# First two experts as 96 float32 slots, one gather per 128 slots, slot counts by rank and 8 KB weight runs in a mixture-of-experts layer

## The chip, the core and the metric

The kernel runs on one core of one Trainium2 chip. The core has five engines that work side by side: TensorE (PE, with its weight loads PEld), VectorE (DVE), ScalarE (ACT), GpSimd (POOL) and SyncE (SP), and 16 DMA engines that move data between the chip's memory and the on-chip buffers. SP issues the plain transfers here, POOL the indirect ones. The metric is the device time of one execution in microseconds (us); lower is better. Each time given is a median of several executions.

## What is computed

One layer on 512 tokens of width D = 1024 in float32: a convolution and a gated linear attention with a layer norm, then a mixture of 16 experts in 4 groups, then a second layer norm. Each token takes the best group, and in it the two best experts, with weights from two softmaxes; an expert is a gated network of hidden width 512.

```python
D_MODEL = 1024; SEQ = 512; N_GROUPS = 4; EXPERTS_PER_GROUP = 4
TOP_K_IN_GROUP = 2; D_EXPERT = 512
def modulate(x, shift, scale):
    return x * (1.0 + scale) + shift
def post_norm_residual(x, y, gate, g, b):
    return layer_norm(DEEPNORM_ALPHA * x + gate * y, g, b)
# of a layer: x = post_norm_residual(x, <mixer>, ...), then
# h = modulate(x, shift2, scale2);  y = sum over a token's two experts e of
#     weight_e * ((silu(h @ w1[e]) * (h @ w3[e])) @ w2[e])
# x = post_norm_residual(x, y, gate2, ln2_g, ln2_b)
```

With the inputs of the reference the 16 experts receive 73, 3, 53, 71, 100, 186, 70, 94, 134, 56, 61, 109, 5, 5, 3 and 1 of the 1024 token places. Experts 0 and 1 are always done first; the other fourteen, sorted by their counts (rank 0 is the fullest), have 186, 134, 109, 100, 94, 71, 70, 61, 56, 53, 5, 5, 3 and 1.

## The kernel before, in words

The first half of the kernel (convolution, attention, first norm, up to about 318 us) is the same in both kernels apart from small loads. The part in question has three stages.

**Routing** (lines 1040 to 1180). DVE works out each token's group, experts and weights; a short product counts the tokens of each expert and gives every token its place in its expert's list (`pos`, `posr`). A *job* is one expert with a fixed number of *slots* (`CAPS`, by rank). For a block of slots `one_hot` builds on DVE a 0/1 matrix of tokens by slots, `slots` multiplies it on PE with a small table `aux` (tile `psl`), which gives each slot its token's row number and weight, and `gather` lets POOL fetch the tokens' rows from memory (`tokd` into `gx`). The first job is another case: `pick` brings its rows to their slots with 64 float32 products on PE with a float32 one-hot (`ohf`), without a gather. Meanwhile the weights of the first two experts come in, and `split` (line 377) cuts them into a high half (`whi`, a cast on ACT, L389) and a low half (`wlo`, a subtraction on DVE or POOL, L391).

**Jobs**, in the order F0, F1 (experts 0 and 1, 128 slots each) and then ranks 12, 0, 11, 6, 10, 1, 3, 8, 4, 2, 5, 9, 7, 13 (`ORDER`). An expert's weights are six pieces of 1 MB (two halves each of w1, w3 and w2), in a ring of twelve buffers. `ev = nc.sync.value_load(...)` reads which expert has the rank, then SP issues six loads; a load waits until the job that used its buffer is through. A job of 128 or more slots is a `BigJob`: rows are transposed on PE, scaled and shifted on DVE and ACT, split into halves (`Xh`, `Xl`), and each product is done as three (high by high, low by high, high by low) with 256 columns in w1 and w3 and 512 in w2. A job of 64 or 32 slots is a `SmallJob` of R = 2 or 4: the columns are spread over R groups of output partitions, in plain float32, without a split. Each block's output is added to its tokens' rows in memory by one indirect transfer on POOL (`scatter`, L1182, `ob` into `yd`); rows of `x1` were put in `yd` before. The loop does `hidden` of a job, the one-hots of a later one, `load` (transposes) of the next, `prep_next` (slots and gather) of the job three on, and then `outputs` (w2 and scatter).

Slots in use beyond a job's count are handled by a loop at the end (`nfb` blocks); with the counts above it has none to do, by either kernel's table.

**Tail**: `finish` reads `yd` back (`yf`), does the second norm, and stores. A scheduler orders the instructions of each engine by dependences and priorities, so the order on an engine is not quite that of the code.

## Time and profile before

| | us |
|---|---|
| Time before, median of 3 runs (702.49 to 704.54) | 704.35 |
| The profiled execution, time | 701.98 |
| The profiled execution, span of the trace | 700.2 |
| from the first product of an expert to the last (343.4 to 670.1) | 326.7 |
| from there to the end | 30.1 |

Times on the trace count from the start of the span; the profiled execution's own time is 1.8 us over its span, and the median of the runs is 2.4 us over that. In the page's first line, a share is the busy time of an engine in the span; the line of DMA gives tenths of the 16 engines' time in 40 slices of 17.5 us each. PEclk is the clock that TensorE was granted, as a share of the full one.

### The profile page before, as it was taken

To read this page: it belongs to the slowest core of one execution; us is meant where nothing else is said; L and a number is where in the kernel's file an instruction comes from. 1 tells how busy PE (TensorE), PEld (TensorE's weight loads), DVE (VectorE), ACT (ScalarE), POOL (GpSimd) and SP (SyncE) were. 2 spreads that over 40 slices of the span, in tenths; PEclk is the share of its full clock that TensorE was granted. 3 is DMA by queue.
4 is the path that set the end of the run, shared out by engine and by line. 5 is a ranking of instruction groups with operands and counts; after the bars stand their busy time and mean duration, and the time that the engine had idled before them with its cause. 6 is when DMAs were issued, how large, how long until landed. Compare 5 with 4: busy or idle time off the path is not lost.

```text
span 700.2 us, 11612 instructions
## 1 busy us (share of the span) xinstructions
PE 645.3 (92%) x4378; PEld 505.8 (72%) x4378; DVE 474.9 (68%) x1036; ACT 318.5 (45%) x505; POOL 135.2 (19%) x106
## 2 busy tenths in 40 slices
PE   5899999989999999996798899998999999999973
PEld 4565689777887787784698598594988588996431
DVE  8545741785965877649899875586669887594245
ACT  3338721458432234325276553454557375471100
POOL 2410000000000100025417312032123221122112
PEclk9999999999999999997799999999999999999998
DMA  8997965372112189626469899899999999979943
GB/s 310 370 338 248 313 197 176 121 230 73 59 62 64 57 294 373 204 91 219 165 204 355 314 338 369 263 369 353 359 367 319 324 369 345 348 216 349 318 142 116
DMA packets 114125, 176.79 MB, mean 252 GB/s; under 512 B 3905, under 2 KB 82129, under 8 KB 114066
## 3 DMA queue, kind: packets, MB, share of 16 engines
q1 hardware_dynamic: 107570, 157.31, 65.4%
q0 software_dynamic: 5136, 15.50, 8.9%
q10 hardware_dynamic: 1360, 3.21, 1.2%
q8 instruction: 36, 0.59, 0.3%
q14 instruction: 23, 0.19, 0.1%
HBM read 160.92 MB, written 15.07 MB: 251 GB/s over the span
## 4 chain that ended last, share of the span: by engine, by line
PE 68%; DVE 17%; ACT 6%; DMA 4%; issue 3%; POOL 1%; DVEq 0%; ACTq 0%
PE pb L144 32%; PE mm L144 21%; PE gl L144 3%; PE pt L154 3%; DVE wlo L391 3%; DMA raw<-in_expert_w_dram 3%; ACT whi L389 2%; PE po L144 2%; PE bg L146 2%; PE tp L154 1%; DVE gg L621 1%; PE pt L144 1%; PE py L144 1%; PE pu L144 1%; DVE gg L620 1%
## 5 line engine op out<-in xcount | busy, mean ns | idle before, releaser
L391 DVE TENSOR_TENSOR wlo<-raw,whi 128x1024 fp32r<-128x1024 f32 x65 | 80.3, 1245 | 50.9 <-ACT whi L389 50.4
L144 PE MATMUL pb<-whi,Xh 128*128 128x256 f32 x384 | 110.6, 289 | 3.7 <-ACT Xh L1205 3.7
L144 PE MATMUL pb<-whi,Xl 128*128 128x256 f32 x384 | 110.2, 288 | 1.6 <-DVE Xl L1206 1.6
L144 PE MATMUL pb<-wlo,Xh 128*128 128x256 f32 x384 | 108.9, 285 | 0.0
L389 ACT CAST whi<-raw 128x1024 fp32r<-128x1024 f32 x68 | 70.9, 1049 | 57.6 <-PE mm L144 26.2
L389 ACT CAST whi<-ew 128x1024 fp32r<-128x1024 f32 x68 | 71.3, 1051 | 29.4 <-PE pb L144 28.2
L144 PEld LDWEIGHTS pb<-whi,Xh 128*128 128x128 f32 x384 | 73.3, 191 | 8.0 <-ACT Xh L1205 7.1
L391 DVE TENSOR_TENSOR wlo<-ew,whi 128x1024 fp32r<-128x1024 f32 x56 | 68.8, 1237 | 12.9 <-ACT whi L389 10.9
L144 PEld LDWEIGHTS pb<-whi,Xl 128*128 128x128 f32 x384 | 73.1, 191 | 2.0 <-DVE Xl L1206 2.0
L144 PEld LDWEIGHTS pb<-wlo,Xh 128*128 128x128 f32 x384 | 73.3, 191 | 0.1
L1182 POOL DMA_INDIRECT yd<-ob,idx x18 | 30.6, 1699 | 103.3 <-DVE ob L1340 31.5
L391 POOL TENSOR_TENSOR wlo<-ew,whi 128x1024 fp32r<-128x1024 f32 x12 | 29.9, 2501 | 86.9 <-issue 70.2
L144 PE MATMUL mm<-hhi,whi 128*128 128x512 f32 x112 | 44.3, 403 | 1.6 <-ACT hhi L368 1.6
L144 PE MATMUL mm<-hhi,wlo 128*128 128x512 f32 x112 | 42.8, 392 | 0.0
L144 PE MATMUL mm<-hlo,whi 128*128 128x512 f32 x112 | 42.5, 390 | 0.0
L294 POOL TENSOR_TENSOR ss<-ss,nhalf 128x4 f32<-128x4 f32 x4 | 5.4, 1357 | 188.8 <-DVE ss L293 188.8
L144 PE MATMUL pb<-wlo,Ah 128*128 128x512 f32 x96 | 38.6, 403 | 0.2 <-DVE wlo L391 0.2
L144 PE MATMUL pb<-whi,Ah 128*128 128x512 f32 x96 | 38.8, 404 | 0.0
L144 PE MATMUL pb<-whi,Al 128*128 128x512 f32 x96 | 38.1, 402 | 0.3 <-DVE Al L1206 0.3
L144 PE MATMUL mm<-wlo,hhi 128*128 128x256 f32 x128 | 36.9, 288 | 0.0
L144 PE MATMUL mm<-whi,hhi 128*128 128x256 f32 x128 | 36.7, 287 | 0.0
L144 PE MATMUL mm<-whi,hlo 128*128 128x256 f32 x128 | 36.6, 286 | 0.0
(418 smaller groups left out, 1445.8 us busy)
## 6 DMA issues: line engine op xcount, KB each, us to landing
ew<-in_expert_w_dram SPq DMA_DIRECT2D x64, 1024.0 KB
raw<-in_expert_w_dram SPq DMA_DIRECT2D x32, 1024.0 KB
raw<-in_w_ada_dram SPq DMA_DIRECT2D x22, 1024.0 KB
raw<-in_w_in_dram SPq DMA_DIRECT2D x10, 1024.0 KB
raw<-in_w_out_dram SPq DMA_DIRECT2D x4, 1024.0 KB
xz<-in_x_dram SPq DMA_DIRECT2D x4, 512.0 KB
ada<-in_w_ada_dram SPq DMA_DIRECT2D x2, 1024.0 KB
x<-in_x_dram SPq DMA_DIRECT2D x4, 512.0 KB
```

The source lines that it names most:

```text
L144: return PE.matmul(o, lhsT, rhs, **kw)
L146: return PE.matmul(o, lhsT, rhs, **kw)
L154: PE.transpose(pool_tile[:, j * P:(j + 1) * P], s, ident)
L294: pows.append(G.tensor_tensor(dst, dst, nhalf[:, :dst.shape[1]], op=OP.pow))
L389: S.copy(hi, r[:, k0:k0 + step, :])
L391: lows.append(lo_eng[k0 // step].tensor_tensor(lo, r[:, k0:k0 + step, :], hi.bitcast(FT), op=OP.subtract))
L620: V.tensor_tensor_scan(g[0:DK, :], mask[0:DK, :n], m[0:DK, :], 0.0, op0=OP.mult, op1=OP.add)
L621: V.tensor_tensor_scan(g[DK:P, ::-1], mask[DK:P, :n], m[DK:P, ::-1], 0.0, op0=OP.mult, op1=OP.add)
L1182: G.indirect_dma_start(out=yd.rearrange("t (r w) -> (t r) w", r=R), out_offset=bass.IndirectOffsetOnAxis(ap=idx[:, :1], axis=0), in_=o, in ...
```

## The change

The change touches the expert part in these ways.

- The first two experts have 96 slots, done as a 64-slot part (R = 2) and a 32-slot part (R = 4) in plain float32; `FirstJob`, `pick` and their splits are gone, and so is POOL's share of the low halves (`POOL_LO`).
- The slot counts by rank go from 256, 256, 256, 128 (four times), 64 (five times), 32, 31 to 256, 192, 128 (three times), 96 (twice), 64 (three times), 32 (three times), 31. In blocks: 12 of 128 slots, 5 of 64 and 2 of 32 become 6 of 128, 8 of 64 and 8 of 32. Jobs whose weights are split go from nine to five.
- Rows come by one gather of whole 4 KB token rows for up to 128 slots, into one of three fixed buffers (`gxs`). After the first two, empty slots hold a row number beyond the table and are skipped. A `SmallBlock` gets the row numbers and weights of its R parts by a small product (`tables`, tile `ptb`).
- A piece of weights is cut so that each partition reads one run of 8 KB; before, a run was 1 KB in w1 and w3 and 4 KB in w2. The contraction index that a partition holds changes with it; transposes take every fourth column (`every`) and the modulation uses a permuted table (`abx`). Products with w1 and w3 are 512 columns wide.
- Jobs run in the order F0, F1, 12, 0, 11, 1, 9, 2, 8, 3, 7, 4, 5, 6, 10, 13. `hidden` is cut into steps; the loop does `load` of the next job ahead of the last step, then `gate` (the activation), `slots` and gather of the job two on, the first step of the next job, and then `outputs` of this one. The rows of the second norm are read at the end into the ring.

```diff
 NS = 2
-CAPS = [256] * 3 + [128] * 4 + [64] * 5 + [32, 31] + [0] * 2
-ORDER = [12, 0, 11, 6, 10, 1, 3, 8, 4, 2, 5, 9, 7, 13]
+FIRST = 96
+CAPS = [256, 192] + [128] * 3 + [96] * 2 + [64] * 3 + [32] * 3 + [31] + [0] * 2
+ORDER = [12, 0, 11, 1, 9, 2, 8, 3, 7, 4, 5, 6, 10, 13]
...
     def piece_src(nm, ev, h):
         src = a[nm][0, ev:ev + 1] if isinstance(ev, int) else a[nm][0, bass.ds(ev, 1)]
-        src = src[:, h * 256:(h + 1) * 256, :] if nm == "expert_w2" else src[:, :, h * 256:(h + 1) * 256]
-        return src.rearrange("o (k p) n -> p (o k) n", p=P)
-
-    RING = ["h8"] * 4 + ["mw"] * 2 + ["raw"] * 4 + ["h8"] * 4 + ["ew"] * 2 + ["mw"] * 2 + ["raw"] * 4
+        n = src.shape[1] // 2
+        src = src[:, h * n:(h + 1) * n, :]
+        return src.rearrange("o (p k) n -> p (o k) n", p=P)
+
+    RING = ["h8"] * 4 + ["mw"] * 2 + ["raw"] * 4 + ["ew"] * 2
...
-        shape = [P, 2, 1024] if nm == "expert_w2" else [P, 8, 256]
-        r = raw8(shape) if tag == "raw" else (e8 if tag == "ew" else h8 if tag == "h8" else m8)(shape, FT, "ew")
+        r = ring_tile([P, 2, 1024] if nm == "expert_w2" else [P, 4, 512])
...
-    V.memset(e0c[:, 0:NS], float(P))
+    V.memset(e0c[:, 0:NS], float(FIRST))
...
-    def gather(idx, R):
-        g = mo.tile([P, D // R], FT, name="gx", tag="gx", bufs=3)
-        ins = G.indirect_dma_start(out=g, out_offset=None, in_=tokd.rearrange("t (r w) -> (t r) w", r=R),
-                             in_offset=bass.IndirectOffsetOnAxis(ap=idx[:, :1], axis=0))
-        return g, ins
...
+    class Group:
...
+            self.n = sum(P // R for R, _ in blocks)
+            self.blocks = [(Block if R == 1 else SmallBlock)(self, R, o) for R, o in blocks]
...
+            pa = pt_("psl")
+            for i in range(NT):
+                mm(pa[:n, :NA], self.oh[:, i, :n], self.auxj(i), start=i == 0, stop=i == NT - 1)
...
+            self.g = gxs[ngx[0] % len(gxs)][:n]
+            ngx[0] += 1
+            kw = dict(bounds_check=T - 1, oob_is_err=False) if ngx[0] > NS else {}
+            self.last = G.indirect_dma_start(out=self.g, out_offset=None, in_=tokd,
+                                             in_offset=bass.IndirectOffsetOnAxis(ap=idx[:, :1], axis=0), **kw)
...
+                for c in range(4):
+                    PE.transpose(pt[:, c * n:(c + 1) * n], every(gh, 4, c), ident[:n, :n])
...
+                    A, B = (abx[:, q, ks, 0:1].to_broadcast([P, 4, n]) for q in range(2))
+                    x = self.xt[:, ks, :n]
+                    V.tensor_tensor(x, v, A, op=OP.mult)
+                    V.tensor_tensor(x, x, B, op=OP.add)
...
+            xh, xl = self.group.X
+            for k in range(4):
+                kc = 4 * c + k
+                mm3(self.H[wi], xh[:, kc, :], xl[:, kc, :], his[k], los[k], kc == 0, kc == KC - 1)
...
+            for k in range(4):
+                for q in range(R):
+                    wi, part_ = divmod(q, gw)
+                    mm(self.ph[q * n:(q + 1) * n, :w], self.group.xt[:, 4 * c + k, self.o:self.o + n],
+                       wts[2 * c + wi][:, k, part_ * w:(part_ + 1) * w],
+                       start=c == 0 and k == 0, stop=c == 1 and k == 3)
...
+    def parts_of(cap):
+        groups, off = [], 0
+        while off < cap:
+            R = next(R for R in (1, 2, 4) if P // R <= cap - off or R == 4)
+            if off % P == 0:
+                groups.append([])
+            groups[-1].append((R, off % P))
+            off += P // R
+        return groups
...
+            for c in range(2):
+                for wi in range(2):
+                    if self.big:
+                        W = split(wts[2 * c + wi], 512)
+                        for b in self.big:
+                            b.products(c, wi, *W)
+                        yield
+                if self.small:
+                    for b in self.small:
+                        b.products(c, wts)
...
-    def pick(hf):
-        pt, grp = pt_(), Bank()
-        for k in range(4):
-            for i in range(NT):
-                ks = slice((4 * hf + k) * P, (4 * hf + k + 1) * P)
-                grp.mm(pt[:, k * P:(k + 1) * P], x1[i][:, ks], ohf[:, i, :])
-        x0b.append(pt)
...
+    for j in seq[:NS]:
+        ohs[j] = hots(j)
+        warm(WARM2, pt_)
+        prep(j)
+    jobs[seq[0]].load()
+    with tc.issue_after(jobs[seq[NS - 1]].last.ins):
+        for g, n in zip(gxs, [FIRST] * NS + [0]):
...
+    for i in range(NT - 2, NT):
+        with tc.issue_after(jobs[seq[NS - 1]].last.ins):
+            G.tensor_tensor(x1[i], x1[i], l1g, op=OP.mult)
+        nc.sync.dma_start(yd[i * P:(i + 1) * P, :], x1[i])
+    load_first(6 * NS)
...
+    run = {seq[0]: jobs[seq[0]].hidden(wts[seq[0]])}
+    next(run[seq[0]])
     for n_, j in enumerate(seq):
...
-        jobs[j].hidden(wts[j])
+
+        rest = range(jobs[j].steps - 1)
+        for q in rest:
+            if q == rest[-1] and jn is not None:
+                jobs[jn].load()
+            next(run[j])
...
-        if n_ + 1 < len(seq):
-            jobs[seq[n_ + 1]].load()
-        prep_next(n_ + 3)
+        jobs[j].gate()
+        if n_ >= NS:
+            jobs[j].tables()
+        if n_ + 3 < len(seq) and n_ + 3 >= NS + 2:
+            ohs[seq[n_ + 3]] = hots(seq[n_ + 3])
+        if n_ + 2 < len(seq) and n_ + 2 > NS:
+            prep(seq[n_ + 2])
...
+        if jn is not None:
+            run[jn] = jobs[jn].hidden(wts[jn])
+            next(run[jn])
...
+        if jn is not None:
             jobs[j].outputs(wts[j])
```

(`.n` is the number of slots of a group; `xt` are the modulated rows, transposed; `gxs` are the three buffers of rows. `ptb` stands in `SmallBlock.table`, which copies the result to a weight and a row number.)

On POOL, at the end of routing (L391 before is the low half of a first expert's weights; L1177 and, after, L1227 are gathers; L1182 and L1187 are scatters), before:

```order
L391 TENSOR_TENSOR wlo<-ew,whi 128x1024 x4
L1177 DMA gx<-tokd,idx 128x1024
L1392 MEMSET mark 128x1
L1454 TENSOR_TENSOR x_2369<-x_2369,l1g 128x1024 x2
L1177 DMA gx<-tokd,idx 128x256
```

and after:

```order
L1227 DMA gx_3110<-tokd,idx 96x1024
L1227 DMA gx_3111<-tokd,idx 96x1024
L1476 MEMSET gx_3110 32x1024
L1476 MEMSET gx_3111 32x1024
L1476 MEMSET gx_3112 128x1024
L1483 COPY rep_3201<-ident 64x128 x2
L1483 COPY rep_3204<-ident 32x128 x4
L1488 MEMSET mark 128x1
L1496 TENSOR_TENSOR x_2394<-x_2394,l1g 128x1024 x2
L1227 DMA gx_3112<-tokd,idx 32x1024
```

The four subtractions are gone from the routing, two gathers stand in their place, and buffers are cleared behind them.

On the same queue, where the first two jobs put their outputs out, before:

```order
L1177 DMA gx_3257<-tokd_2403,idx_3253 128x256
L391 TENSOR_TENSOR wlo_3567<-raw_2911,whi_3566 128x1024
L1182 DMA yd_2404<-ob_3535,idx_3168 640x1024
L391 TENSOR_TENSOR wlo_3600<-raw_2913,whi_3599 128x1024
L1177 DMA gx_3478<-tokd_2403,idx_3475 128x1024
L1177 DMA gx_3491<-tokd_2403,idx_3488 128x1024
```

and after:

```order
L1187 DMA yd_2429<-ob_3457,idx_3213 1280x512
L1187 DMA yd_2429<-ob_3477,idx_3219 2560x256
L1227 DMA gx0_3110<-tokd_2428,idx_3576 128x1024
L1227 DMA gx1_3111<-tokd_2428,idx_3590 128x1024
L1187 DMA yd_2429<-ob_3622,idx_3225 1280x512
L1187 DMA yd_2429<-ob_3642,idx_3231 2560x256
```

Each of the first two jobs now has two scatters, and the gathers of rank 0 stand behind the first pair.

On PE, where a job of 128 slots follows one of 64 (`psl` is the product that gives slots their row numbers, `pt<-ident,gx` are the transposes of gathered rows, products with `Ah` and `Al` are the outputs of the job before the two, `xt` and `at` those of the job of 64), before, about the job of rank 6:

```order
L144 MATMUL psl<-aux,oh 128x6
L144 MATMUL pb<-whi,Ah 128x512
L144 MATMUL pb<-wlo,Ah 128x512
...
L144 MATMUL pb<-raw,xt 64x256 x19
L154 MATMUL pt<-ident,hs 128x128 x2
L144 MATMUL pb<-raw,xt 64x256 x13
L144 MATMUL pb<-ew,at 64x512
L154 MATMUL pt<-ident,hs 128x128 x2
L154 MATMUL pt<-ident,gx 128x128 x4
```

and after, about the job of rank 3 (between the two parts stand the 24 output products of rank 2):

```order
L144 MATMUL psl<-aux,oh 128x6
L144 MATMUL pb<-whi,Ah 128x512
L144 MATMUL pb<-wlo,Ah 128x512
...
L144 MATMUL pb<-whi,Al 128x512
L1253 MATMUL pt<-ident,gx_3112 128x128 x8
L144 MATMUL pb<-ew,xt 64x512 x7
```

Before, the row numbers in these rows are for jobs behind rank 6, whose own rows were gathered a stage earlier; after, they are rank 3's own, and 24 products stand between them and the transposes.

## Rows read from the trace of the kernel before

**Rows 1.** The page: busy time of the engines, DMA by slice, and the DMA queues.

```profile
PE 645.3 (92%) x4378; PEld 505.8 (72%) x4378; DVE 474.9 (68%) x1036; ACT 318.5 (45%) x505; POOL 135.2 (19%) x106
...
DMA  8997965372112189626469899899999999979943
...
q1 hardware_dynamic: 107570, 157.31, 65.4%
q0 software_dynamic: 5136, 15.50, 8.9%
```

**Rows 2.** Stages: start:end us, length, busy us by engine (count), PE clock, DMA share, GB/s.

```profile
343.40:371.10 27.70, 23.05 (x159) 20.79 (x157) 25.74 (x61) 19.60 (x33) 7.89 (x4) 0.94 0.76 264
371.10:394.90 23.80, 21.18 (x142) 18.23 (x143) 23.04 (x38) 14.24 (x17) 15.70 (x7) 0.93 1.07 361
394.90:403.00 8.10, 7.23 (x108) 3.88 (x107) 6.02 (x18) 3.69 (x9) 2.60 (x2) 1.00 0.69 244
403.00:440.20 37.20, 36.98 (x269) 33.95 (x270) 24.89 (x49) 17.78 (x27) 7.73 (x5) 1.00 1.07 358
440.20:453.80 13.60, 13.57 (x93) 6.88 (x92) 5.93 (x11) 5.10 (x11) 1.57 (x1) 1.00 0.85 234
618.50:636.90 18.40, 18.40 (x135) 16.52 (x133) 15.76 (x23) 10.65 (x13) 5.71 (x4) 1.00 1.00 294
636.90:649.20 12.30, 12.27 (x90) 6.66 (x91) 2.61 (x6) 1.30 (x4) 1.70 (x2) 1.00 1.06 352
662.90:670.10 7.20, 6.02 (x99) 3.10 (x98) 1.20 (x3) 1.88 (x4) 1.55 (x1) 1.00 0.39 61
670.10:700.20 30.10, 15.69 (x32) 6.57 (x32) 17.03 (x33) 2.17 (x3) 6.01 (x7) 0.84 0.38 141
```

**Rows 3.** Timeline of DVE in the routing: start us, us, engine, line, operation, tiles.

```profile
321.21 2.06 DVE L1060 TENSOR_TENSOR e1e<-e1e,e1k 128x16 f32<-128x16 f32 x1
326.81 2.33 DVE L1127 CAST aux<-wgt 128x8 bf16<-128x8 f32 x1
329.05 2.44 DVE L1154 TENSOR_SCALAR ohf<-slot,posr 128x128 f32<-128x128 bf16 x1
```

**Rows 4.** Timeline of POOL: start us, us, engine, line, operation, tiles, [idle before, releaser].

```profile
326.64 7.07 POOL L391 TENSOR_TENSOR wlo<-ew,whi 128x1024 fp32r<-128x1024 f32 x3 [3.41 <-ACT whi L389]
...
445.69 1.57 POOL L1182 DMA_INDIRECT yd<-ob,idx  x1 [8.41 <-DMA yd<-ob,idx]
...
457.68 1.48 POOL L1177 DMA_INDIRECT gx<-tokd,idx  x1 [0.30 <-PE pb L144]
```

**Rows 5.** Timeline of PE, at the first job and at rank 1.

```profile
333.99 5.52 PE L144 MATMUL pt<-ohf,x 128*128 128x128 f32 x26 [1.65 <-DVE ohf L1154]
343.44 0.36 PE L144 MATMUL pb<-whi,Xh 128*128 128x256 f32 x1
...
488.88 0.60 PE L154 MATMUL pt<-ident,gx 128*128 128x128 f32 x4
```

**Rows 6.** The gathers (tile gx), time from issue to landing.

```profile
DMA to landing us min/median/max: 4.3/8.2/11.4
```

**Rows 7.** PE groups by form in job 12: form xcount, busy us, mean ns, idle before.

```profile
L144 PE MATMUL pb<-ew,xt 128*32 128x256 f32 x64 | 3.7, 380 | 0.0
L144 PE MATMUL pb<-ew,at 128*32 128x256 f32 x32 | 2.1, 385 | 0.1
```

**Rows 8.** The scatters (line 1182), time from issue to landing.

```profile
DMA to landing us min/median/max: 5.0/9.2/10.9
```

**Rows 9.** DMA from 511 to 520 us, with weights in 1 KB runs alone.

```profile
DMA packets 3102, 3.14 MB, mean 349 GB/s; under 512 B 48, under 2 KB 3101, under 8 KB 3101
```

**Rows 10.** DMA from 521.5 to 526.5 us, with weights in 4 KB runs.

```profile
DMA packets 565, 2.04 MB, mean 408 GB/s; under 512 B 29, under 2 KB 80, under 8 KB 565
```

**Rows 11.** The chain that ended last: start us, us, what.

```profile
664.02 4.96 DMA yd<-ob,idx
668.99 3.86 DMA yf<-yd
```

476 lines of the change are left out of this document (245 added, 231 removed).

## The prediction

> **What bounds the kernel now.** I read the page first, then the stages of the expert part, then the timelines at its start, and the chain at its end. In the page TensorE is busy for 92% of the span, and the slices of DMA are nearly all 9 in the last half [rows 1]. Two resources are thus close to full, and the table by stage says which one sets the end of each stage [rows 2]. In the second job DVE is busy for 23.04 of 23.8 us: the halves of the weights are the limit there. In rank 0 (256 slots, 403.0 to 440.2) PE is busy for 36.98 of 37.2 us, in rank 5 (618.5 to 636.9) for 18.40 of 18.40, in rank 9 (636.9 to 649.2) for 12.27 of 12.3. From rank 0 on PE is the bound, and DMA runs close beside it (share 1.07 in the first of these). So what takes work from PE is worth its full time, as long as DMA doesn't become the limit: the ring is twelve pieces deep, and a job's own weights were loaded two jobs ahead.
>
> Ahead of the jobs, DVE works through the routing. Three of its instructions there take 2.06, 2.33 and 2.44 us [rows 3], where others of the same lines take 0.17 to 0.3; each lies beside POOL's subtractions, of which three take 7.07 us together [rows 4]. The first job's rows then come to their slots by float32 products on PE, the last 26 of them 5.52 us long, and the first product of an expert starts at 343.44 [rows 5].
>
> **Start of the jobs.** POOL's subtractions leave the routing, so the stretched instructions should fall to about 0.2 us. The first, ahead of the one-hots, is 1.9 us on the path. The later ones (6.5 us with a fourth like them) stood beside the float32 one-hot that `pick` waited for; that chain goes as a whole. In its place come the row numbers (a short product and four small DVE instructions, about 1 us), a gather, eight transposes and the modulation. The gather landed after 4.3 to 8.2 us (least and median) [rows 6]; at this point the queues are nearly idle, but rows are read in full, and in the rows the lowest value is one of 18. One-hots and `aux` are ready by about 326, row numbers by 328, rows by 332 to 336, and with 2 to 4 us for transposes and modulation the first product comes at 335 to 340. I take 338, near the upper end, since this path has no row of its own; it gives 5.4 us.
>
> **Jobs.** Prices by rows: a 64-slot job took 13.6 and 12.3 us [rows 2]; I take 13.0. A 32-slot job took 8.1 and 7.2 us [rows 2]; I take 7.5 alone. As part of a 96-slot job only its products count, 3.7 + 2.1 = 5.8 us [rows 7], so 96 slots cost 13.0 + 5.8 = 18.8. That holds for F0 and F1 too, which took 27.7 and 23.8 us [rows 2], and now need no split at all. A 128-slot job takes 18.4, a 256-slot one 37.2 [rows 2]. For 192 slots I add a 128 and a 64 that shares its weights: 18.4 + 12.3 = 30.7. The products with 512 columns do the same columns in half the instructions; I cost them alike. The sum: four of 96, 75.2; one of 256, 37.2; one of 192, 30.7; three of 128, 55.2; three of 64, 39.0; four of 32 or 31 slots, 30.0; together 267.3 us, where the stage took 326.7. What goes: F0 and F1 together (51.5 - 37.6 = 13.9), rank 1 as 192 slots instead of 256 (6.5), rank 2 as 128 instead of 256 (18.8), ranks 10 and 11 as 32 instead of 64 (11), and the short waits inside stages. Ranks 5 and 6 (96 slots instead of 128) gain nothing by these prices.
>
> The small product of `tables` and its two DVE instructions come sixteen times, beside other work on PE that is not waiting for them; with 0.1 us of PE each they are within the rounding. DVE has 24 pieces fewer to take low halves of, as jobs with a split go from nine to five, and the twelve instructions that POOL did come to it; it is not the bound of any stage after F1 [rows 2], so I cost that at nothing. If it were bound in a 128-slot job (15.76 of 18.40 us now [rows 2]), a few us would be lost; the range holds that.
>
> **The clock at the start.** F0 now waits for a gather with little on PE. In F0 and F1 the granted clock was 0.94 and 0.93 [rows 2], that is about 3.3 us at the lower of the two levels (1.2 instead of 2.4 GHz) in F0. If PE starts F0 at the lower level and stays there for some 8 us, that costs 4 us; ends: 1.7 (as now) and 9 (nearly the whole of F0). I add 4.
>
> **Waits for gathers.** Before, rows were gathered long ahead: a gather at 457.68 [rows 4] was used by transposes at 488.88 [rows 5]. Now slots and gather stand behind `gate`, and only the first step of the next job and the outputs of this one lie between them and the transposes. At ranks 3 and 4 that is 24 products of 512 columns: a third of the columns of an 18.4 us stage [rows 2], about 5.6 us. At rank 0, 6 and 13 I count, by the same rate, about 6.5, 8.5 and 6 to 7 us. Against that the row numbers take about 1 us and a gather 8.2 in the median, 11.4 at most [rows 6]; with the steps between engines, some 10 us. The stalls come to 4.5 for rank 0 (with 1 us more, as it has two gathers), 4.4 each for ranks 3 and 4, 1.5 for rank 6 and 3 for rank 13: 18 us. At the other nine jobs a full small or large job lies between. Ends: 0, if a gather lands in 4.3 us; 36, if it takes 11.4 and more jobs wait. 18 lies between and uses the median.
>
> **The end.** Scatters go from 18 to 21, and one waits for the one before (8.41 us idle on POOL [rows 4]). The last job's neighbours now are small: their scatters come at 7.5 us apart, less than the 9.2 us that one takes to land [rows 8]. I add 2 us to the end (0 to 10). The tail is unchanged, 30.1 us [rows 2].
>
> **Is DMA the bound then?** From about 347.5, when F0's first buffers come free, 84 pieces of 1.049 MB have to come. In 1 KB runs the queue moved 349 GB/s [rows 9], in 4 KB runs 408 [rows 10]. With 8 KB runs I take 408: 2.57 us for a piece, 216 us. Gathers and scatters took 62 us of the 16 engines' time for 15.5 MB (8.9% of 700.2 [rows 1]); of these some 10.7 MB fall here, 43 us. Then the last piece comes at 606.5, and with 6 us of work behind it at 612.5, against 338 + 267.3 + 4 + 18 = 627.3 for PE. DMA is close to it, but not the later one.
>
> **The sum.** 338 + 267.3 + 4 + 18 = 627.3; + 30.1 + 2 = 659.4 as span; + 1.8 for the profiled execution's time over its span, and + 2.4 for the median over that execution, as before: 663.6, forecast **663.5 us**. That is 40.8 us (5.8%) below 704.35.
>
> **Rivals.** *Gathers land in time.* With a landing of 4.3 us, the smallest row [rows 6], no job waits: 663.6 - 18 = 645.5. For it: full rows make fewer packets than pieces of rows. Against it: weights in flight fill every engine, and the median was 8.2 with the same load.
>
> *Runs of 8 KB are no faster than 1 KB.* The row of 408 GB/s lasts for 5 us and may flatter. At 349 GB/s 84 pieces take 252.5 us, so the last one comes at 347.5 + 252.5 + 43 = 643, with 6 behind it 649, and 649 + 32.1 + 4.2 = 685. For it: share 1.00 or more in most stages. Against it: two rows at different lengths of run, with the share alike. A rule of the Trainium skill speaks for this rival: "DMA: Bandwidth & Descriptors", Specifications, puts the least transfer for line rate at 512 B, and a core's share of the memory at about 358 GB/s; by that 1 KB runs would already be at the line rate, and the time would be an estimated 679. The row of 408 GB/s speaks against it.
>
> *Slower: the chain of scatters on POOL.* All 21 go one at a time through one queue, gathers stand between them in order, and the tail cannot start before the last has landed. Each costs 1.6 us of issue [rows 4], about 1 us of a gather beside it, and its landing L. The first is ready at about 363; the end is later than now if the last lands after 669 [rows 11], that is from (669 - 363) / 21 = 14.6, or L = 12 us, on; above the 10.9 us of the slowest row [rows 8]. At L = 13 the last one lands at 363 + 21 x 15.6 = 690.6, and with 31.2 behind it [rows 11] and 4.2 the time is 726. For it: longer weight packets stand ahead of a scatter's own on each engine. Against it: with L = 9.2 [rows 8] the chain ends at 611, long before PE. The Trainium skill ("DMA: Bandwidth & Descriptors", Queues, rings and completion order) has each DMA engine go round the queues packet by packet, which is the way in which longer packets would lengthen L; no row shows how much.
>
> **How the numbers follow.** Chances: the forecast, which the ends of its own terms move between 648 and 690 (stalls 0 to 36, clock, scatters), 0.60; gathers in time, 0.18; runs no faster, 0.12; scatters, 0.10, of which 0.08 lie clearly above L = 12 us and 0.02 at it. From the third I put 0.01 with the slower, for both limits at once. A range from 643 to 692 leaves out the scatters and the outer parts of the others, some 0.2. Faster by over 0.3%: 0.60 + 0.18 + 0.11 = 0.89; slower by over 0.3%: 0.08 + 0.01 = 0.09; within 0.3%, about what a measurement of this kernel can tell from no change: 0.02.
>
> **What would show it.** In the profile of the changed kernel: the first product at about 338, and the DVE instructions of the routing at 0.2 us; stages without a wait at 18.8 (96 slots), 30.7 (192), 13 (64) and 7.5 (32); DMA at 400 GB/s or more where only weights move; PE idle some 4 us ahead of the transposes of ranks 0, 3 and 4; scatters on POOL that wait for the one before in the last jobs, and a last landing some 31 us before the end. The prediction is wrong if stages are longer with PE busy (products of 512 columns or the 96-slot jobs dearer than the rows say), if DMA pieces take 3 us each, or if DVE is busy throughout a stage.

## The result, and the profile after

| | us |
|---|---|
| Kernel before, median of 4 runs (702.49 to 704.54) | 703.76 |
| Changed kernel, median of 4 runs (733.35 to 739.21) | 735.6 |
| Ratio, with its 95% interval | 1.0459 (1.0413 to 1.0505) |
| Forecast (range) | 663.5 (643 to 692) |

A run more than 1.5% above the fastest of its kernel counts as slow and is left out of medians and ratios; of all the runs in this document that concerns four of the ten of e8.

The change makes the kernel 4.6% slower, where 5.8% faster was forecast. The profiled execution took 739.21 us (span 737.4). The page of the changed kernel, the lines that answer to [rows 1], with the line of the granted clock:

```profile
PE 648.9 (88%) x3966; PEld 429.0 (58%) x3966; DVE 408.0 (55%) x1008; ACT 250.5 (34%) x417; POOL 103.9 (14%) x106
...
PEclk8799989999999999997798899899897989999788
DMA  8995955362122098353569798857995989616963
...
q1 hardware_dynamic: 46130, 157.31, 57.5%
q0 software_dynamic: 5440, 11.27, 7.0%
```

The same 157.31 MB now need 46130 packets instead of 107570, DVE has 67 us less to do, and PE has fewer instructions. Yet PE is busy a little longer, the slices of DMA in the last half are no longer all 9, and the clock is below 9 tenths in many slices of the expert part. No engine has a larger share of its span busy than before; the work waits.

Stages of the changed kernel, which answer to [rows 2] (start:end, length, busy us by engine PE, PEld, DVE, ACT, POOL with counts, PE clock, DMA share, GB/s). The first line is the whole of the jobs, from the first product of an expert to the last; the others are F0's first step with its transposes, one job of 96 slots (from F1's transposes to rank 12's), rank 0's start, rank 3's start, the last job and the tail:

```profile
346.76:706.00 359.24, 313.77 (x1908) 174.54 (x1908) 173.62 (x434) 105.26 (x178) 58.62 (x44) 0.91 0.78 283
...
344.07:360.56 16.49, 15.33 (x68) 6.04 (x68) 12.02 (x42) 0.00 (x0) 8.65 (x11) 0.54 0.20 77
360.56:380.68 20.12, 20.12 (x179) 9.50 (x175) 3.51 (x8) 5.55 (x14) 0.71 (x1) 1.00 0.67 262
403.60:432.69 29.09, 27.15 (x160) 19.35 (x160) 13.32 (x31) 12.08 (x22) 4.67 (x3) 0.88 0.88 330
550.28:575.68 25.40, 23.25 (x84) 12.68 (x84) 15.99 (x57) 10.81 (x16) 2.55 (x2) 0.80 0.66 224
...
679.48:706.00 26.52, 15.95 (x176) 9.66 (x176) 3.42 (x16) 1.64 (x6) 4.67 (x3) 0.81 1.02 394
706.00:737.40 31.40, 15.44 (x32) 6.60 (x32) 16.84 (x33) 2.17 (x3) 6.02 (x7) 0.79 0.37 136
```

And the same stretch of jobs in the kernel before, for comparison of its clock and busy time:

```profile
343.40:670.10 326.70, 311.89 (x2311) 250.60 (x2309) 233.52 (x468) 168.11 (x258) 87.74 (x49) 0.99 0.99 323
```

The jobs took 359.2 us instead of 326.7, and the forecast had 289.3 for them (267.3 of work, 18 of waits, 4 for the clock). Three parts make the 69.9 us over the forecast. **Idle:** PE is idle for 359.24 - 313.77 = 45.5 us, 27.5 over the 18. **Clock:** a mean of 0.91 between levels of 1 and one half (2.4 and 1.2 GHz) is 18% of the stretch, 65 us, at the lower one. If PE was busy all that time, half of it, 32 us, was lost: up to 28 over the 4. **Work:** 313.77 - 32 = 282 us of PE at the full clock at the least, 14 over the 267.3. Outside the jobs the first product came 8.8 us later than forecast (346.76 instead of 338), the tail was 0.7 us shorter, and what lies between span and median was 6.0 us less than I had added. Together that is 69.9 + 8.8 - 0.7 - 6.0 = 72.0, the miss. The last of these is no work: the profiled execution is the longest of the four, 3.6 us above their median, where the sum reckoned with one 2.4 below, so up to 6 us of the other parts are a difference between executions and not between kernels.

PE's waits from 344 to 706 (who waited for what: us in total, times, longest; the 4.8 us ahead of F0's transposes are among them), then four of them in the timeline of PE, which answer to [rows 5]:

```profile
PE pt L1253 <- DMA gx<-tokd,idx: 31.7, 7, 7.4
PE pb L144 <- DMA raw<-in_expert_w_dram: 8.2, 2, 7.0
PE pb L144 <- ACT Xh L1264: 6.2, 3, 2.1
```

```profile
344.07 1.53 PE L1253 MATMUL pt<-ident,gx 96*128 96x96 f32 x8 [4.83 <-DMA gx<-tokd,idx]
...
529.02 1.22 PE L1253 MATMUL pt<-ident,gx 64*128 64x64 f32 x8 [7.36 <-DMA gx<-tokd,idx]
...
550.28 1.96 PE L1253 MATMUL pt<-ident,gx 128*128 128x128 f32 x8 [4.61 <-DMA gx<-tokd,idx]
...
595.42 1.95 PE L1253 MATMUL pt<-ident,gx 128*128 128x128 f32 x8 [4.52 <-DMA gx<-tokd,idx]
```

The bracket is the idle time before and what ended it. The waits stand ahead of transposes of gathered rows, ranks 3 and 4 within 0.3 us of the forecast 4.4. Rank 0 waited 7.0; ranks 8 and 5, for which I had forecast none, 7.36 and 2.93; ranks 6 and 13, for which I had 1.5 and 3, hardly at all (0.4 for rank 13). The eight transposes at 550.28 and 595.42 take 1.95 us; eight of the same kind without a wait took 1.23 at 503.12, so those behind a wait run at a lower clock. The stages behind the waits of ranks 0, 8, 3 and 4 have a mean clock of 0.80 to 0.88. It is no rule without exception: rank 5's stage stayed at 1.00 behind its 2.93 us, and rank 1's (454.21 to 482.49) had 0.88 behind 2.12 us of waiting for `Xh`.

Rank 8's wait comes out of the order on POOL. In the timeline of POOL:

```profile
502.90 1.59 POOL L1187 DMA_INDIRECT yd<-ob,idx  x1 [8.25 <-DVE ob L1320]
516.76 1.57 POOL L1187 DMA_INDIRECT yd<-ob,idx  x1 [12.27 <-DMA yd<-ob,idx]
518.63 1.00 POOL L1227 DMA_INDIRECT gx<-tokd,idx  x1 [0.30 <-issue]
```

The scatter of 516.76 waits for that of 502.90 to land, and the gather stands behind both in the queue; it landed 10.35 us later, at 529.0. Its row numbers were ready at 511.3 (DVE, L1223), so the 7.3 us until its issue are as long as the whole wait. Over the whole run landings were these, in us, gathers first and then scatters (they answer to [rows 6] and [rows 8]):

```profile
DMA to landing us min/median/max: 2.5/6.7/12.3
```

```profile
DMA to landing us min/median/max: 4.9/9.1/13.1
```

The end of the jobs, in the chain that ended last (start us, us, what; it answers to [rows 11]), and SP's queue ahead of it (start us, us):

```profile
647.09 0.31 PE ptb L144 x2
...
664.20 4.92 DMA yd<-ob,idx
...
669.97 8.71 DMA yd<-ob,idx
...
679.80 9.69 DMA yd<-ob,idx
...
690.22 8.82 DMA yd<-ob,idx
...
699.80 7.75 DMA yd<-ob,idx
707.56 3.58 DMA gx<-yd
```

```profile
646.19 0.33 SPq L1556 DMA_DIRECT2D l1b<-in_ln_b_dram  x1
646.77 0.36 SPq L1019 DMA_DIRECT2D ew<-in_expert_w_dram  x1
667.81 2.51 SPq L1561 DMA_DIRECT2D obw<-l1b  x4
670.58 2.81 SPq L1019 DMA_DIRECT2D ew<-in_expert_w_dram  x5
```

The first line, one product of `tables` in its two rows, is for later. Five scatters, issued one after another, lead to the read-back at 707.56. On SP two small groups of transfers block the weights. They belong to `last_hot`, which prepares the last job's share of the tail. It fetches a bias into a tile `l1b` of tag "ob", one of the two buffers that outputs use, and spreads it into `obw`. The diff moved its call from the last job but one (`n_ == len(seq) - 2`) to the fourth from the end (`len(seq) - 4`), with a line that my prediction passed over. The first waits for that buffer from 626.5, when SP had issued the load ahead of it, to 646.19. Eleven pieces of weights are issued only after 668, the first five of them in the last line; hence the two waits for `raw`, 8.2 us.

### The profile page after: what moved, and what is told of

Same layout as the page of the kernel before. It is cut to its first block, busy times and chain, and to the rows that moved or that the text cites. A ratio compares the mean times of both kernels' runs of the same rounds, so it can differ in the third digit from the quotient of the medians.

```text
span 737.4 us, 10628 instructions
## 1 busy us (share of the span) xinstructions
PE 648.9 (88%) x3966; PEld 429.0 (58%) x3966; DVE 408.0 (55%) x1008; ACT 250.5 (34%) x417; POOL 103.9 (14%) x106
## 3 DMA queue, kind: packets, MB, share of 16 engines
q1 hardware_dynamic: 46130, 157.31, 57.5%
## 4 chain that ended last, share of the span: by engine, by line
PE 57%; DMA 17%; DVE 10%; issue 8%; ACT 5%; POOL 1%; ACTq 0%; SPq 0%; DVEq 0%; POOLq 0%
PE pb L144 22%; PE mm L144 19%; DMA yd<-ob,idx 7%; DMA gx<-tokd,idx 6%; PE gl L144 3%; PE pt L1253 2%; DVE wlo L398 2%; PE bg L146 2%; PE po L144 2%; PE tp L154 1%; DMA x<-in_x_dram 1%; ACT whi L396 1%; DMA raw<-in_w_ada_dram 1%; DVE gg L640 1%; PE bg L160 1%
## 5 line engine op out<-in xcount | busy, mean ns | idle before, releaser
L144 PE MATMUL pb<-ew,xt 128*32 128x256 f32 (+1 forms) x480 | 73.7, 495 | 1.4 <-DVE xt L1270 1.2
L1187 POOL DMA_INDIRECT yd<-ob,idx x21 | 33.9, 1614 | 143.7 <-DVE ob L1388 50.4
L1253 PE MATMUL pt<-ident,gx 128*128 128x128 f32 (+3 forms) x144 | 24.8, 325 | 31.7 <-DMA gx<-tokd,idx 31.7
L144 PE MATMUL pb<-ew,at 128*32 128x256 f32 (+1 forms) x384 | 51.4, 477 | 0.9 <-DVE at L1371 0.5
L144 PE MATMUL pb<-whi,Xh 128*128 128x512 f32 x96 | 42.2, 439 | 6.2 <-ACT Xh L1264 6.2
L144 PE MATMUL pb<-raw,xt 128*32 128x256 f32 (+1 forms) x288 | 38.8, 480 | 8.2 <-DMA raw<-in_expert_w_dram 8.2
L1253 PEld LDWEIGHTS pt<-ident,gx 128*128 128x128 f32 (+3 forms) x144 | 21.3, 215 | 39.0 <-issue 28.9
L1227 POOL DMA_INDIRECT gx<-tokd,idx x18 | 20.1, 1114 | 164.1 <-issue 47.0
L144 PEld LDWEIGHTS pb<-ew,xt 128*32 128x32 f32 (+1 forms) x480 | 22.4, 127 | 33.7 <-issue 26.2
L144 PE MATMUL pb<-whi,Xl 128*128 128x512 f32 x96 | 41.1, 428 | 0.0
L144 PE MATMUL pb<-wlo,Xh 128*128 128x512 f32 x96 | 41.0, 427 | 0.0
```

The source lines that it names most:

```text
L144: return PE.matmul(o, lhsT, rhs, **kw)
L1187: G.indirect_dma_start(out=yd.rearrange("t (r w) -> (t r) w", r=R), out_offset=bass.IndirectOffsetOnAxis(ap=idx[:, :1], axis=0), in_=o, in ...
L1227: self.last = G.indirect_dma_start(out=self.g, out_offset=None, in_=tokd, in_offset=bass.IndirectOffsetOnAxis(ap=idx[:, :1], axis=0), **kw)
L1253: PE.transpose(pt[:, c * n:(c + 1) * n], every(gh, 4, c), ident[:n, :n])
```

## The experiments

Each time is a median on the same chip as runs of the kernel before; the ratio is to those.

| kernel | us | ratio (95%) |
|---|---|---|
| e1_gather_ahead | 706.19 | 1.0055 (1.0014 to 1.0097) |
| e2_order_end | 747.73 | 1.0638 (1.0575 to 1.0702) |
| e3_both | 718.70 | 1.0223 (1.0153 to 1.0293) |
| e4_warm | 715.37 | 1.0198 (1.0121 to 1.0274) |
| e5_last_hot | 730.15 | 1.0360 (1.0296 to 1.0425) |
| e6_ahead_last_hot | 699.57 | 0.9962 (0.9927 to 0.9997) |
| e7_three | 709.01 | 1.0098 (1.0071 to 1.0125) |
| e8_three_perm0 | 704.90 | 1.0024 (0.9987 to 1.0060) |
| e9_ob_of_four | 689.83 | 0.9815 (0.9773 to 0.9856) |
| e10_first128 | 707.72 | 1.0056 (1.0038 to 1.0074) |
| e11_caps128 | 696.23 | 0.9922 (0.9891 to 0.9954) |
| e12_runs_1k | 703.35 | 1.0003 (0.9973 to 1.0033) |
| e13_ob4_alone | 730.93 | 1.0390 (1.0365 to 1.0416) |
| e14_ob4_caps128 | 692.42 | 0.9865 (0.9818 to 0.9912) |
| e15_ob4_old_order | 690.48 | 0.9828 (0.9805 to 0.9852) |

**Gathers one job further ahead.** To the changed kernel:

```diff
-        if n_ + 3 < len(seq) and n_ + 3 >= NS + 2:
-            ohs[seq[n_ + 3]] = hots(seq[n_ + 3])
-        if n_ + 2 < len(seq) and n_ + 2 > NS:
-            prep(seq[n_ + 2])
+        if n_ + 4 < len(seq):
+            ohs[seq[n_ + 4]] = hots(seq[n_ + 4])
+        if n_ + 3 < len(seq):
+            prep(seq[n_ + 3])
```

> The changed kernel with slots and gather of a job done one job earlier (three jobs on instead of two), as the kernel before had it; nothing else is different. Theory 1, lead: in the changed kernel PE idles 31.7 us in all ahead of the transposes of gathered rows (7 waits, the longest 7.4), and after most of these waits the granted clock is 0.80 to 0.88 over the stage, which I put at another 20 us. Then all waits but the first job's 4.8 go, the clock in rank 0 to rank 5 is 0.97 or more, and the time falls by 35 to 47 us to 688 to 700. Rival, queue: the gathers land late because POOL's queue and the DMA engines are full, so an earlier issue only moves the wait; then the idle time ahead of transposes stays above 20 us and the time falls by less than 10 us. Rival, end: what is gained is lost at the end, where the scatters of the last jobs go one at a time; then the time falls by 20 to 30 us and the last five scatters follow each other without a gap of PE work.

It gave 706.19, 29 us less than the changed kernel. PE's waits in the jobs, and the whole of the jobs (columns as above):

```profile
PE pb L144 <- ACT Xh L1264: 10.3, 3, 6.0
...
PE pt L1253 <- DMA gx<-tokd,idx: 4.6, 1, 4.6
```

```profile
341.00:671.00 330.00, 306.80 (x1908) 171.83 (x1908) 172.47 (x436) 105.06 (x178) 58.37 (x45) 0.93 0.84 308
```

All waits for gathers but F0's are gone, 27 us of them, and that is most of what came back. The gather's place is thus the largest single cause of the miss. It is not the whole: the run is still slightly behind the kernel before. Nor did the clock come back with these waits, as the first theory had it: its mean is 0.93 instead of 0.91, and by the same estimate as above some 23 us are still lost to it instead of 32. Other waits have grown (`Xh` from 6.2 to 10.3 us), and the clock is low behind them: 0.89 in rank 0, 0.83 in rank 1, and 0.76 in the last job, behind its weights. So the gain of 29 lies below the 35 to 47 of that theory, in the range of the rival on the end.

**The order at the end.** Rank 4, the last job of 128 slots, between ranks 10 and 13, so that its work covers the small jobs' scatters:

```diff
-ORDER = [12, 0, 11, 1, 9, 2, 8, 3, 7, 4, 5, 6, 10, 13]
+ORDER = [12, 0, 11, 1, 9, 2, 8, 3, 7, 5, 6, 10, 4, 13]
```

> The changed kernel with rank 4 (128 slots) done between ranks 10 and 13 instead of ahead of rank 5; only the order table is different. Theory, end: the last 43 us of the changed kernel's jobs are set by five scatters one at a time (at 664.2, 670.0, 679.8, 690.2 and 699.8) and by the weights of the last job, for which PE waits 8.2 us; 18.4 us of PE work between the small jobs and the last one hides both, and the time falls by 8 to 14 us to 722 to 728. Rival: PE's work is only moved, and the wait for the gather of rank 4 moves with it; then the time stays within 4 us of 735.6.

It made it worse, by 12 us. PE in that run:

```profile
679.70 0.79 PE L144 MATMUL pb<-wlo,Xh 128*128 128x512 f32 x1 [7.81 <-DVE wlo L398]
```

A large job's low halves are late at 680. The high half that goes with them is there in time (PE uses it at 670.10), but DVE waits from 670.5 to 677.62 for an output buffer that a scatter holds, and makes the low half only then. The next piece of that job's weights stands behind the blocked transfers of `last_hot` on SP; ACT gets it at 674.04, after 6.25 us of waiting. Together with the earlier gathers (e3, both diffs) the order was a loss too, 12.5 us over e1, where neither of the two expectations had it:

> Both edits together: gathers one job earlier, and rank 4 between ranks 10 and 13. If the two losses are independent, the time falls by the sum of the two, some 50 us, to 680 to 692, below the kernel before. If the gathers only hide the end (PE is early, the scatters are as late as ever), the time is that of the first edit within 4 us.

**The clock of F0.** Products without use ahead of F0's transposes, on top of e3:

```diff
         prep(j)
+    warm(40, pt_)
     jobs[seq[0]].load()
```

> As the run with both edits, and 40 more idle transposes on PE (0.123 us each, 4.9 us) between the row numbers of the first two jobs and the transposes of the first job, where PE idles 4.8 us in the changed kernel; they add no result. Theory, clock: the first job runs at a granted 0.54 over 16.5 us because PE idled ahead of it; with PE kept busy it is 0.9 or more, and the time is 5 to 8 us less than that of the run with both edits. Rival: DVE and the weights set the first job's pace and not the clock; then the time is the same within 2 us.

It gave 715.37 against 718.70, within the intervals of the two, and between what theory and rival had. The windows of e4 (columns as above):

```profile
340.00:343.50 3.50, 1.64 (x12) 1.36 (x11) 3.49 (x14) 0.00 (x0) 2.85 (x7) 1.00 0.10 36
343.50:346.00 2.50, 2.50 (x8) 1.39 (x10) 2.50 (x6) 0.00 (x0) 2.36 (x3) 0.73 0.00 0
346.00:351.00 5.00, 3.60 (x14) 0.94 (x12) 4.90 (x19) 0.00 (x0) 3.02 (x3) 0.50 0.52 210
```

PE comes to F0 at the full clock, and F0's transposes (339.76 to 340.94) still have it. Behind them PE idles 1.73 us for the modulation, then does the two-column products of `tables` and the first of F0's own, and the clock falls to 0.50. So the wait ahead of F0 is not what holds the clock down, or not alone; what does, I can't say from these runs.

**The transfers of `last_hot`** where the kernel before has them, alone (e5) and with the earlier gathers (e6):

```diff
-        if n_ == len(seq) - 4:
+        if n_ == len(seq) - 2:
             ohT, obw = last_hot()
```

> The changed kernel with the preparation of the last job's rows (last_hot, which puts five small transfers on SP) back at the second last job, where the kernel before had it, instead of four jobs ahead of the end; nothing else is different. In the changed kernel SP issues no weights from 626 to 670 us but one piece: the first of the five transfers waits for a buffer that a scatter holds, and the other four for ACT, and the last eleven pieces of weights stand behind them. Theory, two chains: both this queue and the five scatters, one at a time, from 664.2 to 707.5 end the jobs at the same time (the last product ends at 705.6), so that one alone gains little; SP then issues the last weights by 650, the waits for weights at the end (8.2 us) go, the scatters stay where they are, and the time falls by at most 5 us, to 730 or more. Rival, queue alone: the scatters only look tight since PE was late; the time falls by 10 us or more.

> Gathers one job earlier, and the preparation of the last job's rows at the second last job. By the theory of two chains the last scatter lands where it did (about 672 on the trace), and the time is within 5 us of the 706.2 of the run with earlier gathers alone. By the rival it falls by 10 to 15 us, as the waits for weights at the end (8.3 us) and the low clock after them (0.76 over the last 28 us) go.

Alone it gave 5.5 us (the intervals overlap a little), about what the theory of two chains had; on top of e1 it gave 6.6, between the 5 of that theory and the 10 of its rival. SP no longer stands still, and the waits for weights are gone in both. That the scatters at the end keep the rest is argued from e5, where the last of them is issued at 696.55 instead of 699.80, and the routing begins 3.7 us earlier too. In e6 another wait is seen, among the waits of DVE:

```profile
DVE ob L1388 <- DMA yd<-ob,idx: 6.9, 2, 4.5
DVE ohl L1179 <- DMA yd<-ob,idx: 6.4, 1, 6.4
```

DVE writes an output tile `ob` only when one of the two buffers is free, and a scatter holds its buffer until it has landed. What stands behind on DVE (halves, modulation, activations) waits with it.

**The order once more**, with both of these mended (e7), and then with the extra products of the first half at another priority (e8):

> The three edits together: gathers one job earlier, the last job's preparation at the second last job, and rank 4 between ranks 10 and 13. By the theory of two chains, now both are taken away: the weights of rank 4 and of the last job come in time (PE waited 11.6 us there in the run with the first and the third edit), the scatters of ranks 5, 6 and 10 lie beside the 18 us of rank 4, and the time falls to 685 to 695, below the kernel before. If the order costs time in itself, it stays at 705 or above.

> As the run with three edits, and the 4 small products that make the permuted table of the modulation no longer ahead of the others by priority. In the changed kernel they stand at 89.3 us, right behind 1.3 us of idle PE and 8 narrow products; the granted clock then is 0.50 for 6.5 us, where the kernel before stays at 1.00, and PE is 4.3 us later from there on. Theory, clock: with the small products elsewhere the clock stays at 1.00 at that place and the time is 3 to 5 us less than that of the run with three edits. Rival: the products only fall in another thin place, or hold up the next loads, and the time is the same within 2 us.

The order still costs 9 us over e6, as the second expectation of e7 had it, so the blocked weights were not its only price; I did not follow it further. The diff of e8 to e7 (`columns` makes the table by which rows are modulated):

```diff
-        def columns(src, bias):
+        def columns(src, bias, prio=prio):
...
-            return ts_, lambda: columns(lambda j: s.rearrange("r (p c) -> r c p", c=4)[:, j], perm)
+            return ts_, lambda: columns(lambda j: s.rearrange("r (p c) -> r c p", c=4)[:, j], perm, 0)
```

e8 is 4.1 us shorter than e7, by the ratios, whose intervals don't overlap, 0.7%: inside the 3 to 5 us of the theory. But the reason is not the one that it gave. In e7 the clock was 0.57 from 92 to 100 and 1.00 from 150 to 170; in e8 it was 1.00 and 0.83. A fall from 1 to 0.57 over 8 us and one to 0.83 over 20 us lose the same, 3.4 us of PE each ((1 - 0.57) x 8 and (1 - 0.83) x 20): that part of the loss only moved. The moved products now stand at 119.33, with the clock at 1.00 around them; the new fall follows 1.99 us of idle PE and eight other narrow products at 161.55, where e7 idled 0.50 us. What else made e8 shorter isn't shown; of the 4.6 us by which its `gm` (the start of the choice of experts) is earlier than e7's, 3.5 are there before either set of products.

**Output buffers.** To e6, the outputs of 32-slot parts get two buffers of their own, for which the tag "s" gives up one of three:

```diff
-            s_ = mo.tile([P, 512], FT, name="s", tag="s", bufs=3)
+            s_ = mo.tile([P, 512], FT, name="s", tag="s", bufs=2)
...
-            hs = mo.tile([P, 512], FT, name="hs", tag="s", bufs=3)
+            hs = mo.tile([P, 512], FT, name="hs", tag="s", bufs=2)
...
-            ob = mo.tile([P, ow], FT, name="ob", tag="ob", bufs=2)
+            ob = mo.tile([P, ow], FT, name="ob", tag="ob" if R == 2 else "ob4", bufs=2)
```

> Base of this and the next three: gathers one job earlier and the last job's preparation at the second last job (699.6 us, 0.996 of the kernel before). Here the outputs of 32-slot parts get two buffers of their own, so that a job of 96 slots with two scatters doesn't hold both output buffers; to make room the buffers for the activation go from three to two. In the base DVE waits 6.9 us for the landing of scatters ahead of outputs and 6.4 us ahead of the last one-hot, all of DVE's later work stands behind, and PE waits 5.7 us in rank 0 (for Xh) and 6.2 us in the last job. Theory, scatters hold DVE: these waits go, with the low clock behind them, and the time falls by 8 to 14 us, to 0.976 to 0.985 of the kernel before. Rival: rank 0 waits for its weights anyway and the end waits for the scatters themselves; the time falls by less than 3 us.

689.83, 9.7 us below e6 and 1.9% below the kernel before, as the theory had it: the shortest of all. The wait of DVE and PE's largest remaining one:

```profile
DVE ob L1388 <- DMA yd<-ob,idx: 1.7, 1, 1.7
```

```profile
PE pb L144 <- ACT Xh L1264: 6.3, 3, 2.2
PE pt L1253 <- DMA gx<-tokd,idx: 5.0, 1, 5.0
```

The same edit alone, on the changed kernel:

> The changed kernel with its outputs of 32-slot parts in two buffers of their own (tag ob4; the tag s gives up one of its three buffers for it), and nothing else. Theory (output buffers held by scatters block DVE, but in the changed kernel most of that time lies inside the waits for gathers, which the edit doesn't touch): 728 to 736 us, at most 1% under the changed kernel's 735.6. Rival (the held buffers cost their 10 us in any setting, as they did with the gathers ahead): 722 to 727 us.

730.93, 4.7 us below the changed kernel (the intervals just touch): the held buffers cost about half as much where the gathers are waited for anyway. Waits that lie one behind the other hide each other here, and what an edit gives depends on which of them are still there.

**Parts of the change undone or resized.** On e6: the first experts with one block of 128 slots and a split (e10; two lines that keep sizes in step are left out here), ranks 5 and 6 with 128 slots (e11), and w1 and w3 in 1 KB runs (e12):

```diff
-FIRST = 96
+FIRST = 128
```

```diff
-CAPS = [256, 192] + [128] * 3 + [96] * 2 + [64] * 3 + [32] * 3 + [31] + [0] * 2
+CAPS = [256, 192] + [128] * 5 + [64] * 3 + [32] * 3 + [31] + [0] * 2
```

```diff
-        d = nc.sync.dma_start(r, piece_src(nm, ev, h))
+        s = piece_src(nm, ev, h)
+        for c in (range(1) if nm == "expert_w2" else range(2)):
+            w = 1024 if nm == "expert_w2" else 256
+            d = nc.sync.dma_start(r[:, :, c * w:(c + 1) * w], s[:, :, c * w:(c + 1) * w])
```

> The base with the first two experts as 128 slots with split weights again (one scatter each), their rows still by a gather. By the prices of the prediction (18.8 us for 96 slots, 27.7 and 23.8 for the split ones) the time rises by 12 to 16 us, to 1.013 to 1.02 of the kernel before. Theory, scatters and clock eat it: F0 in plain float32 runs at a clock of 0.57 and four scatters of the two jobs hold DVE, so that the 128-slot form costs no more than 5 us, 1.003 of the kernel before or less.

> The base with 128 slots for ranks 5 and 6, as before the change: one scatter each instead of two, a split of their weights, about the same work on PE (18.4 us each by a row of the kernel before, 20.0 for 96 slots by the changed one). Theory, scatters set the end: the last chain of scatters is three instead of five, the last one lands 8 us or more earlier than 672, and the time falls by 5 to 12 us. Rival, PE sets the end: the time is within 3 us of the base.

> The base with every piece of w1 and w3 fetched by two transfers of half its columns, so that the runs are 1 KB as before the change (w2 stays at 8 KB runs); the data and all the products are the same. Weights alone then move at about 349 GB/s as in the kernel before, not 424: 56 pieces take 3.0 us instead of 2.5, 28 us more in all. Theory, DMA is close to the bound: DMA is busy without a gap from 500 to 620 us in the base, so some 10 to 25 us of it show in the time (1.01 to 1.03 of the kernel before). Rival: PE is the bound through and through, and the time rises by less than 4 us.

The first experts with 128 slots cost 8.1 us more (intervals apart), so that part of the change is a gain, though less than the 12 to 16 by the prices of the prediction. Ranks 5 and 6 with 128 slots took 3.3 us less, with intervals that overlap. With 1 KB runs it was 3.8 us more, with intervals that overlap a little, where 10 to 25 were expected if DMA were close to the bound. The windows from 500 to 560 us of e6 and then of e12:

```profile
500.00:560.00 60.00, 57.77 (x256) 34.82 (x254) 42.09 (x109) 28.91 (x43) 10.75 (x8) 0.94 1.02 374
```

```profile
500.00:560.00 60.00, 55.03 (x239) 33.76 (x239) 39.95 (x102) 26.01 (x37) 10.38 (x7) 0.91 1.08 346
```

At a share above 1 in both, the long runs moved 374 GB/s and the short ones 346.

**On the shortest version**, e9, the same slot counts as in e11, and the order of jobs of the kernel before:

```diff
-ORDER = [12, 0, 11, 1, 9, 2, 8, 3, 7, 4, 5, 6, 10, 13]
+ORDER = [12, 0, 11, 6, 10, 1, 3, 8, 4, 2, 5, 9, 7, 13]
```

> The fastest version so far (gathers a step ahead, small last weights two jobs before the end, own output buffers for 32-slot parts; 689.8 us) with ranks 5 and 6 as 128 slots instead of 96. Theory (a 96-slot job costs 20.0 us of PE and a 128-slot job 18.4, and one output less per job spares a scatter; it gave 3.3 us without the output buffers): 685 to 688 us. Rival (the 3.3 us were relief for the output buffers, which are now there anyway, so nothing is left): 689 to 691 us.

> The fastest version so far (689.8 us) with the order of jobs of the kernel before (12, 0, 11, 6, 10, 1, 3, 8, 4, 2, 5, 9, 7, 13) in place of the changed one. Theory (small and large jobs take turns in the changed order; in the old one two large jobs stand side by side four times, which needs weights faster than DMA brings them and leaves small jobs' scatters elsewhere in a row): 692 to 700 us. Rival (order is worth nothing once gathers and outputs don't wait): 688 to 691 us. Second rival (the changed order is itself a part of the loss): under 687 us.

Both came out where the rivals had them, or above: 692.42 and 690.48, with intervals that overlap that of e9. With free output buffers two jobs of 128 slots bring nothing over two of 96, and the order of the kernel before is worth as much as the changed one, when gathers and outputs don't wait. The order of e2 wasn't tried there.

## Why the prediction was wrong, step by step

**Right.** The routing: from the first instruction of the choice of experts (`gm`, at 318.79 before and 328.75 after) to the first product it took 24.6 us before and 18.0 after, a gain of 6.6 where 5.4 was forecast. The gathers' new place as a wait: it is there, at ranks 0, 3 and 4, and it is the largest cause. That ranks 5 and 6 gain nothing from 96 slots (e14). That DMA was not the later limit (e12). Long runs are moved at a higher rate: 374 against 346 GB/s, and 394 in the last job. A rule of the Trainium skill, "DMA: Bandwidth & Descriptors", Specifications, by which 1 KB is at the line rate already, differs from these rows. In the time the rows hardly show: e12 is 3.8 us longer than e6, with intervals that overlap. The median landing of scatters (9.1 us) is what it was before.

**Waits for gathers: 18 us, measured 26.9** (31.7 less F0's 4.8, which the start has). The term was in its bounds of 0 to 36. The step that failed is the one that let a full job between gather and use count as cover: rank 8 waited 7.36 us, because its gather was issued late, behind a scatter that waited for another, and rank 5 waited 2.93. I counted landing times, and not what stands ahead of a gather in POOL's queue. Rank 0 waited 7.0 where I had 4.5; that ranks 6 and 13 did not take their 4.5 hides a part of the error.

**The clock: 4 us, measured up to 32.** I costed the lower clock once, in F0, and none behind the waits that I had forecast myself. F0's first step ran at 0.54 for 16.49 us, which alone is about 7.5 us, inside my end of 9. Most of the rest stands behind waits, at 0.80 to 0.88 in the stages shown, and comes back as waits of every kind go, not those for gathers alone: the mean of the jobs is 0.91 here, 0.93 in e1, and 0.97 in e9, whose jobs have little waiting. At up to 28 us over the forecast this is as large a part of the miss as the idle time, and I had put it at nothing outside F0. Why F0 itself stays low is open (e4).

**The jobs' work: 267.3 us, measured 282 or more.** Windows of e9's jobs and tail:

```profile
343.90:652.10 308.20, 298.29 (x1908) 167.39 (x1908) 173.28 (x433) 105.09 (x178) 58.12 (x43) 0.97 0.89 329
652.10:689.20 37.10, 16.71 (x34) 7.03 (x32) 17.08 (x33) 2.17 (x3) 7.56 (x8) 0.75 0.37 123
```

There 6% of 308.2 us are at the lower clock, some 9 us lost, so 298.3 - 9 = 289 us are work. The table by stage shows 20.12 us, all busy at the full clock, for a job of 96 slots that I priced at 18.8. Part of it are small products, by form, in the changed kernel's jobs (count, busy us, mean ns, idle before):

```profile
L1253 PE MATMUL pt<-ident,gx 32*128 32x32 f32 x32 | 4.5, 281 | 0.4 <-DMA gx<-tokd,idx 0.4
L144 PE MATMUL ptb<-sa,rep 32*128 32x2 f32 x16 | 3.6, 295 | 0.0
L144 PE MATMUL ptb<-sa,rep 64*128 64x2 f32 x16 | 3.5, 284 | 1.1 <-DVE at L1371 1.1
```

Whole rows need eight transposes for a group however few its slots: 4.5 / 4 = 1.1 us for 32 slots, where rows gathered in four parts had needed a quarter as many. And the sixteen products of `tables`, each of which the trace has as two rows, are 7.1 us busy; the rows overlap, and in the chain of waits above one product takes 0.31, so on the path the sixteen are about 16 x 0.31 = 5.0 us, where the forecast had 0.1 each, 1.6 in all. I took the price of a product from its size, and not from a row of one as narrow. The rest of the 14 to 22 us isn't apportioned.

**The first half: nothing, measured +10 us.** `gm` begins at 318.79 before, at 328.75 after, and from 322.73 to 331.64 in the other runs of the changed kernel. "Apart from small loads", as I put it ahead of the prediction, is not so: the permuted table `abx` needs a second set of products (`bg<-sel,adas`), which stand in the first half. The products `mm` begin shortly before them and end well behind; the line of one kind of them (count, ns of one at least, median and most, first and last start, form), before, after and in e8:

```profile
L144 PE MATMUL mm<-whi,hhi x128: 279/283/467, 80.6 to 159.7; 128*128 128x256 f32 x128
```

```profile
L144 PE MATMUL mm<-whi,hhi x128: 278/283/559, 85.8 to 168.9; 128*128 128x256 f32 x128
```

```profile
L144 PE MATMUL mm<-whi,hhi x128: 278/283/387, 81.2 to 158.9; 128*128 128x256 f32 x128
```

So 5.2 of the 10 us are there at 85.8 already, ahead of the new products. This part differs between runs with the same first half (e1 begins `mm` at 81.6), and nothing here shows how much of it is the change. The stretch of `mm` is 79.1 us before and 83.1 after, 4 us more. In e1, PE's timeline and one window there:

```profile
89.29 1.92 PE L146 MATMUL bg<-sel,adas 128*128 128x8 f32 x8
```

```profile
90.00:92.00 2.00, 2.00 (x10) 2.00 (x10) 0.75 (x10) 0.00 (x0) 0.00 (x0) 0.50 1.06 335
```

Just before, from 88 to 90, the clock was 0.99, and it is 0.50 until 96. In the kernel before it is 1.00 there. All fifteen profiles with the products at this place have a fall to 0.50 between 88 and 100; e8, which has them elsewhere, has none, and its `mm` take 77.7 us. So the products' place brings this fall. But e8 lost as much at 162, so that the 4 us were not to be had by moving them there.

**The end and the scatters.** The rival that was slower priced the chain as one total: from L = 12 us at every scatter on. L was 9.1 in the median, so by that rule it should not have bitten; it bit in places. A scatter that waits for another keeps a gather behind it (rank 8), keeps an output buffer and with it DVE (9.7 us between e6 and e9), and five in a row close the jobs (664.2 to 707.6). "Their scatters come at 7.5 us apart, less than the 9.2 us" was counted as 2 us. In the changed kernel the blocked weights covered it, in e9 it stands alone: its tail is 37.1 us against 30.1 before, so 7 where 2 was forecast: its last scatter lands 6.3 us behind the last product.

**SP's queue: not in the sum.** `last_hot` before the last jobs' weights cost 5.5 to 6.6 us (e5, e6). The test "is DMA the bound" compared totals and took the transfers to be issued when buffers come free; the share of DMA fell to 0.13 between 654 and 668 because the queue's head waited.

**What e9 leaves of the miss.** 689.83 - 663.5 = 26.3 us: the first product 5.9 later than 338, the jobs 18.9 longer than 289.3, the tail 5.0 longer than 32.1, less 3.6 outside the span. PE is idle for 9.9 us in those jobs, so most of the 18 us of waits are gone, and work and clock have taken their place and more. Of the 40.8 us of the forecast, 13 are to be had with the three mends of e9 (702.92 - 689.83, on the same chip).

**The range.** The ends of the terms (waits 0 to 36, clock 1.7 to 9, scatters 0 to 10) span 641 to 695 when they are added, not the 648 to 690 that the prediction gives for them. The measured time lies outside either, since large parts of what made it were no terms of the sum: the clock behind waits, the waits for weights, and the first half.
